# Where attention's results are read back to, and where one weight's low part comes from

## The chip, the cores and the metric

The kernel runs on one core of a Trainium2 chip. The metric is the device time of one execution in microseconds (us), less is better. TensorE is written PE (PEld is its weight load), VectorE DVE, ScalarE ACT, GpSimd POOL; SyncE, SP, issues the DMA transfers.

## The reference

One layer of a streaming encoder works on 1056 frames (1024 of a prompt and 32 of a sample) of 1024 features. Cut to what matters:

```
h  = rms_norm(x, g_mix);  z = h @ w_in            # q, k, v, ch, cb, cc, ga, gb
a  = window_attention(q, k, v) @ w_attn_out
bo = (cb * causal_conv3(cc * ch)) @ w_conv_out
x  = x + (sigmoid(ga) * a + sigmoid(gb) * bo) @ w_mix_out
x  = x + cross_attention(rms_norm(x, g_cross) @ w_cq, mem_k, mem_v) @ w_co
x  = x + square(relu(rms_norm(x, g_mlp) @ w_up)) @ w_down
```

A final norm follows. All inputs and results are float32.

## The kernel before, in words

Features lie on the 128 partitions, in eight groups (k on the input side of a product, f on the output side); frames run along a tile. The frames are cut into chunks c = 0, 1, 2 of 384, 384 and 288. To keep float32 accuracy on PE, every operand is held as a high part (its float32r rounding, by an ACT cast) and a low part (operand minus high part, a DVE subtract). A product of a 1024-feature input therefore takes 24 matmuls for one f and one chunk: for each k the weight's high part `wh` with the input's high part (L200), `wh` with the input's low part (L201) and the weight's low part `wl` with the input's high part (L202).

**Weights.** A list of steps is written out by hand, and each step names the weight it needs (`item`, `plan`, `worder`). `fetch_w` loads a 128 x 1024 weight (512 KB) into one of two raw tiles `wr` (L159); `issue_w` makes `wh` and `wl` from it (ACT L129, then DVE L130), up to three weights ahead. The weights of the output projections are used once for each chunk. For some of them, listed in the dictionary `kept`, the low part is written to HBM at the first use (`wl_d`, L179); at later uses only the cast is done (L173), and `wl` is read back from `wl_d` (L172). `w_conv_out` 1 is one of these.

**Stage 1, attention's output product.** Attention has stored its results in HBM (`ao_d`). `open_y` closes attention's memory pools and opens, in their memory, the gate pool `gb` (tags Gb0, Gb1 and Gb2 of five slots each) and the pools of the split operands `Y`. `load_attended(c, k)` reads group k of chunk c back and splits it: a DMA on SP (L788), a cast (L790), a subtract (L791). The read lands in a temporary tile `ct`, one of six (`NCT`) that the whole kernel shares. Chunk 0's eight reads come first; chunk 1's eight and the first four of chunk 2 are hung behind the three chunks of a gate product, and gates for chunk 2 follow (`gate_a2`, f = 2, 3, 4, with products in `pa` and results in Gb2). Then `do_attn_out(f)` takes f = 0 to 7; behind its first chunk at f = 0 hang the last four reads of chunk 2. Its product is scaled (L826) and stored (L827), or copied (L830). From f = 1 on, reads of the input use Gb0 and Gb1 (`gx_load`, L844); until then these two tags are empty, as the first gates live in another pool, `Ga`.

**Stage 2, the trunk.** Per chunk, `do_conv_out(c, f)` for eight f (DVE L1066 multiplies by the gate, POOL L1067 adds), then `do_mix(c, f)` for eight f (a read of x, L1077; L1081 adds it to the product; L279 and L280 scale and split, L276 sums squares on POOL), then cross attention. `do_conv_out(1, 0)` stands between chunk 0's conv products and its mix products; `do_conv_out(1, 1)`, the second use of `w_conv_out` 1, is the first step after chunk 0's last mix product. While the mix products run, reads and splits of cross attention's keys and values (L1092, L1105, L1097, L1109) are hung in between.

What is pinned keeps its written order; the rest is set by the language's scheduler, which decides on each engine's order from a model of time. Each engine, and SP's queue of DMA issues, works strictly in its order.

Of the kernel before, what the change touches and what calls it, by code (L numbers as in the profile page):

```python
# [10 lines left out]
F32 = mybir.dt.float32  # L11
# [11 lines left out]
CH = [(0, 384), (384, 384), (768, 288)]  # L23
# [17 lines left out]
def hybrid_step(ctx: ExitStack, tc: tile.TileContext, io):  # L41
# [5 lines left out]
    def nm(s):  # L47
        uid[0] += 1
        return f"{s}_{uid[0]}"
# [47 lines left out]
    def pin(ins):  # L97
        return tc.keep_in_program_order(ins)
# [6 lines left out]
    def tmp(n, dt=F32):  # L105
        return tp.tile([P, n], dt, tag="ct", bufs=NCT, name=nm("ct"))

    def slot(pool, tag, n, dt=F32R, bufs=None):
        return pool.tile([P, n], dt, tag=tag, bufs=bufs, name=nm(tag))
# [3 lines left out]

    plan, worder, kept = [], [], {}

    def item(fn, *keys):
        plan.append((fn, keys))
# [8 lines left out]
    def split(hi, lo, src):  # L128
        act.copy(hi, src)  # L129
        dve.tensor_sub(lo, src, hi.bitcast(F32))  # L130
# [16 lines left out]
    def fetch_w(raw=None):  # L147
        if raw is not None:
            pass
        elif third:  # L150
            third["n"] += 1
        if raw is not None:
            pass
        elif third and third["n"] % 3 == 0:
            raw = third["pool"].tile([P, 4, 256], F32, tag="ws", name=nm("wr3")).rearrange("p q c -> p (q c)")
        else:
            raw = wp.tile([P, 1024], F32, tag="wr", bufs=2, name=nm("wr"))
        src = weight(worder[wpos[0] + len(fetched)])
        load = sp.dma_start(raw.rearrange("p (i c) -> p i c", i=4) if len(src.shape) == 3 else raw, src)  # L159
        if third and third["n"] == 3 and third["pool"] is W["pool"]:  # L160
            pin(load)
        fetched.append(raw)

    def issue_w(pieces=(slice(0, 1024),)):
        if not fetched:
            fetch_w()
        raw = fetched.pop(0)
        key = worder[wpos[0]]
        hi = wp.tile([P, 1024], F32R, tag="wh", name=nm("wh"))
        lo = wp.tile([P, 1024], F32R, tag="wl", name=nm("wl"))  # L170
        if kept.get(key) is not None:
            sp.dma_start(lo.bitcast(F32), kept[key])  # L172
            act.copy(hi, raw)  # L173
        else:
            for at in pieces:
                split(hi[:, at], lo[:, at], raw[:, at])
            if key in kept:
                kept[key] = dram.tile([P, 1024], F32, name=nm("wl_d"))
                sp.dma_start(kept[key], lo.bitcast(F32))  # L179
        ready.append((worder[wpos[0]], (hi, lo)))  # L180
        wpos[0] += 1

    def next_w(key):
        while len(ready) <= LOOK and wpos[0] < len(worder) and worder[wpos[0]] is not STOP:
            issue_w()
        k, w = ready.pop(0)
        assert k == key, (k, key)
        return w
# [106 lines left out]
    def norm_x():  # L295
# [45 lines left out]
        with tc.manual_schedule(engines={mybir.EngineType.Activation, mybir.EngineType.DVE}):  # L341
            parts(0, range(1))
            issue_w((slice(0, 256), slice(256, 1024)))
            parts(0, range(1, NF))
            act.copy(ones_r, ones.to_broadcast([P, P]))
            issue_w()
            issue_w()
            squares(0)
# [115 lines left out]
    def do_K(pr, extras=()):  # L464
        def fn(w):
            kt = at_tile([P, NT], F32, "kt")
            ktt[pr] = kt
            for c, (o, n) in enumerate(CH):
                a = acc_tile([P, n])
                gemm(a, w, xg[c])  # L470
                dve.tensor_mul(kt[:, o : o + n], a, R[c])
                after(extras, c)
            sp.dma_start(io["o_k"][pr], kt[:, 896:])

        return fn
# [22 lines left out]
    def do_Q(kv, j, extras=()):  # L498
        def fn(w):
            for c, (o, n) in enumerate(CH):  # L500
                npr = min(n, NPR - o)
                if j == 0:
                    qs[kv, c] = at_tile([P, 4, npr], F32R, "QA" if c < 2 else "QB", 2 if c < 2 else 1)
                    if n > npr:
                        qs[kv, 3] = at_tile([P, 4, n - npr], F32R, "QC")
                a = acc_tile([P, n])
                gemm(a, w, xg[c])
                t = tmp(n)
                dve.scalar_tensor_tensor(t, a, 0.125, R[c], op0=ALU.mult, op1=ALU.mult)
                parts = [(qs[kv, c], slice(0, npr))]  # L510
                if n > npr:
                    parts.append((qs[kv, 3], slice(npr, n)))
                for q, s in parts:
                    for e in range(2):
                        own, other = slice(64 * e, 64 * e + 64), slice(64 - 64 * e, 128 - 64 * e)
                        h = 2 * j + e
                        act.copy(q[own, h], t[own, s])
                        dve.tensor_sub(q[other, h], t[own, s], q[own, h].bitcast(F32))
                after(extras, c)

        return fn
# [145 lines left out]
    G = {}  # L667
# [10 lines left out]
    def do_gate(to, extras=()):  # L678
        def fn(w):
            for c, (o, n) in enumerate(CH):  # L680
                a = acc_tile([P, n])
                gemm(a, w, xg[c])
                t = gate_slot(c, 0)
                dve.tensor_mul(t, a, R[c])
                act.activation(t, t, AF.Sigmoid)
                to(c, t)
                after(extras, c)

        return fn
# [61 lines left out]
    for i, h in enumerate(hosts):  # L751
# [16 lines left out]
        if h[0] == "Q":  # L768
            fn, key = do_Q(h[1], h[2], extras), qt(h[1], h[2])
        elif h[0] == "K":  # L770
            fn, key = do_K(h[1], extras), ("w_in", 8 + h[1])
        elif h[0] == "G":
            fn, key = do_gate(lambda c, t: sa.__setitem__((c, 0), t), extras), ("w_in", 34)
        else:
            fn, key = do_conv(*h, extras), conv_w(h[1], h[0])
# [7 lines left out]
    def yslot(c):  # L783
        return slot(Y[c if c < 2 else "top"], f"Y{c}", CH[c][1])

    def load_attended(c, k):
        t = tmp(CH[c][1])
        pin(sp.dma_start(t, ao_d[c][k // 2][:, k % 2]))  # L788
        hi, lo = aop[c][k] = (yslot(c), yslot(c))
        pin(act.copy(hi, t))  # L790
        pin(dve.tensor_sub(lo, t, hi.bitcast(F32)))  # L791
# [217 lines left out]
    item(open_y)  # L1009
    hold = lambda c, t: sg[c].__setitem__(0, t)  # L1010
    ao = lambda c, ks: [lambda k=k: load_attended(c, k) for k in ks]
    item(lambda: [e() for e in ao(0, range(NF))])
    b0 = [(0, e) for e in ao(1, range(4))] + [(1, e) for e in ao(1, range(4, NF))] + [(2, e) for e in ao(2, range(4))]
# [1007 lines left out]
```

## Time and profile before

| | |
|---|---|
| median of 3 runs | 1748.65 us (1747.12 to 1750.77) |
| profiled execution | 1748.9 us, its span 1746.4 us |
| granted TensorE clock | 0.998 |
| busy: PE, DVE, ACT, POOL | 99%, 68%, 49%, 34% |
| DMA | 346.60 MB, mean 198 GB/s |

Times of rows are in us from the start of the span. In a timeline row stand the start, the duration, engine, line, operation and output <- input; [idle before <- releaser] says how long the engine stood before it and what ended that, and xN joins N instructions in a row, whose first names the shape. A row of the waits names the waiting engine, its tile and line, what it waited for, and the total, the number and the longest. Stage 1 runs from about 540 to 650 us; the place in stage 2 is at 869.

### The profile page before, as it was taken

What the parts mean: (1) busy time and instruction counts of PE and PEld (TensorE: products, weight loads), DVE (VectorE), ACT (ScalarE), POOL (GpSimd) and SP (SyncE); (2) the same over time, 40 slices, a digit from 0 to 9 for tenths busy, and PEclk for the clock granted to TensorE, in tenths of its full rate; (3) what the DMA queues carried; (4) which work ended last, traced back from release to release, by engine and by line L of the source; (5) the groups of instructions that cost most, each with busy time, mean ns of one, the idle gap of its engine ahead of it and who ended that gap; (6) DMA issues with size and microseconds to landing.
All of it is one profiled execution on the core that took longest, in us unless ns stands there. A gap on an engine that the chain in (4) does not pass through costs nothing. (4 is left out here: it accounts for less than half of the span.)

```text
span 1746.4 us, 32603 instructions
## 1 busy us (share of the span) xinstructions
PE 1725.4 (99%) x12262; PEld 1708.0 (98%) x12262; DVE 1192.7 (68%) x2276; ACT 852.7 (49%) x1660; POOL 593.6 (34%) x667
## 2 busy tenths in 40 slices
PE   9999999999999999999999999999999999999998
PEld 8999999999999999999999999999999999999998
DVE  7776776867676656545677888787666686545675
ACT  8653533535335324434556666765444453333444
POOL 0026366453643444452225232005555410000121
PEclk9999999999999999999999999999999999999999
DMA  4333344333436888877766667775767695555555
GB/s 185 99 129 125 119 133 145 121 134 134 156 127 209 288 294 274 281 231 232 270 222 199 217 225 242 234 258 191 222 223 222 217 321 187 189 192 171 191 170 160
DMA packets 179854, 346.60 MB, mean 198 GB/s; under 512 B 18657, under 2 KB 101249, under 8 KB 179569
## 3 DMA queue, kind: packets, MB, share of 16 engines
q1 hardware_dynamic: 163504, 290.07, 50.5%
q0 software_dynamic: 15568, 53.68, 8.8%
q8 instruction: 96, 1.57, 0.4%
q10 hardware_dynamic: 624, 0.77, 0.1%
q14 instruction: 62, 0.50, 0.1%
HBM read 250.73 MB, written 93.14 MB: 197 GB/s over the span
## 5 line engine op out<-in xcount | busy, mean ns | idle before, releaser
L129 ACT CAST wh<-wr 128x1024 fp32r<-128x1024 f32 (+1 forms) x214 | 223.8, 1046 | 369.3 <-PE acc L1808 124.7
L130 DVE TENSOR_TENSOR wl<-wr,wh 128x1024 fp32r<-128x1024 f32 (+1 forms) x214 | 276.4, 1292 | 126.9 <-ACT wh L129 126.2
L200 PE MATMUL acc<-X,wh 128*128 128x384 f32 (+1 forms) x864 | 281.5, 326 | 0.0
L201 PE MATMUL acc<-X,wh 128*128 128x384 f32 (+1 forms) x864 | 278.6, 322 | 0.2 <-DVE X L280 0.2
L202 PE MATMUL acc<-X,wl 128*128 128x384 f32 (+1 forms) x864 | 277.8, 322 | 0.0
L276 POOL TENSOR_TENSOR xacc<-xacc,ct 128x384 f32<-128x384 f32 (+1 forms) x56 | 76.6, 1370 | 379.5 <-ACT ct L274 377.8
L201 PEld LDWEIGHTS acc<-X,wh 128*128 128x128 f32 x864 | 162.7, 188 | 1.5 <-DVE X L280 0.5
L200 PEld LDWEIGHTS acc<-X,wh 128*128 128x128 f32 x864 | 162.4, 188 | 0.9
L202 PEld LDWEIGHTS acc<-X,wl 128*128 128x128 f32 x864 | 162.4, 188 | 0.1
L200 PE MATMUL acc<-Y,wh 128*128 128x384 f32 (+1 forms) x432 | 139.4, 325 | 4.0 <-DVE ct L1066 2.9
L202 PE MATMUL acc<-Y,wl 128*128 128x384 f32 (+1 forms) x432 | 139.2, 323 | 1.8 <-DMA wl<-wl_d 1.8
L201 PE MATMUL acc<-Y,wh 128*128 128x384 f32 (+1 forms) x432 | 139.1, 323 | 0.0
L129 ACT CAST PTh<-pt 128x512 fp32r<-128x512 f32 (+3 forms) x94 | 45.8, 517 | 112.9 <-PE pt L598 111.6
L1807 PE MATMUL acc<-n,wh 128*128 128x264 f32 x352 | 100.2, 285 | 0.0
L1809 PE MATMUL acc<-n,wl 128*128 128x264 f32 x352 | 100.0, 285 | 0.2 <-DVE wl L130 0.2
L1808 PE MATMUL acc<-n,wh 128*128 128x264 f32 x352 | 100.1, 284 | 0.0
L735 POOL TENSOR_TENSOR ws<-ws 128x256 f32<-128x256 f32 x100 | 90.9, 909 | 5.6
L735 POOL TENSOR_TENSOR xacc<-xacc 128x256 f32<-128x256 f32 x100 | 88.9, 889 | 5.7 <-DMA xacc<-in_w_in 0.4
L200 PEld LDWEIGHTS acc<-Y,wh 128*128 128x128 f32 x432 | 80.8, 188 | 5.5 <-DVE ct L1066 3.8
L202 PEld LDWEIGHTS acc<-Y,wl 128*128 128x128 f32 x432 | 81.1, 188 | 2.2 <-DMA wl<-wl_d 2.2
L201 PEld LDWEIGHTS acc<-Y,wh 128*128 128x128 f32 x432 | 81.1, 188 | 0.1
L584 ACT ACTIVATE S<-S,nmx 128x257 f32<-128x257 f32 (+1 forms) x132 | 64.2, 488 | 18.9 <-DVE nmx L579 17.6
(432 smaller groups left out, 5553.7 us busy)
## 6 DMA issues: line engine op xcount, KB each, us to landing
wr<-in_w_up SPq DMA_DIRECT2D x53, 512.0 KB, 4.4
wr<-in_w_in SPq DMA_DIRECT2D x52, 512.0 KB, 3.6
wr<-wsum_d SPq DMA_DIRECT2D x40, 512.0 KB, 3.6
wr<-in_w_conv_out SPq DMA_DIRECT2D x24, 512.0 KB, 3.9
wr<-in_w_mix SPq DMA_DIRECT2D x24, 512.0 KB, 5.0
wr<-in_w_down SPq DMA_DIRECT2D x24, 512.0 KB, 4.1
n_d<-Z SPq DMA_DIRECT2D x32, 264.0 KB, 4.3
xacc<-in_w_down POOLq DMA_DIRECT2D x16, 512.0 KB, 4.6
```

What stands on the lines that cost most here:

```text
L129: act.copy(hi, src)
L130: dve.tensor_sub(lo, src, hi.bitcast(F32))
L200: pe.matmul(out, wh[:, a], hi, start=(k == 0), stop=False)
L201: pe.matmul(out, wh[:, a], lo, start=False, stop=False)
L202: pe.matmul(out, wl[:, a], hi, start=False, stop=(k == len(acts) - 1))
L276: pool_e.tensor_tensor(acc, acc, sq, op=ALU.add)
L584: act.activation(stl[:, h, : nk + 1], stl[:, h, : nk + 1], AF.Exp, scale=-1.0, bias=nmx[:, h : h + 1], accum_out=den[:, h : h + 1],)
L735: pin(pool_e.tensor_tensor(t[:, to], t[:, x], t[:, y], op=ALU.add))
L1807: pe.matmul(a, wh[:, s], hi, start=(t == 0 and k == 0), stop=False, skip_group_check=True)
L1808: pe.matmul(a, wh[:, s], lo, start=False, stop=False, skip_group_check=True)
L1809: pe.matmul(a, wl[:, s], hi, start=False, stop=(t == 1 and k == 7), skip_group_check=True)
```

## The change

In stage 1, reads of chunk 1 land in slots of Gb1 and those of chunk 2 in the first 288 columns of slots of Gb0, both idle then, instead of the six shared tiles. Chunk 0 stays with those. In the weights, a count of uses is kept; the second use of `w_conv_out` 1 forms its low part with the subtract L130, and only its third use reads it back.

```diff
-    plan, worder, kept = [], [], {}
+    plan, worder, kept, uses = [], [], {}, {}
...
-        if kept.get(key) is not None:
+        uses[key] = uses.get(key, 0) + 1
+        if kept.get(key) is not None and (key != ("w_conv_out", 1) or uses[key] == 3):
             sp.dma_start(lo.bitcast(F32), kept[key])
             act.copy(hi, raw)
         else:
             for at in pieces:
                 split(hi[:, at], lo[:, at], raw[:, at])
-            if key in kept:
+            if key in kept and uses[key] == 1:
                 kept[key] = dram.tile([P, 1024], F32, name=nm("wl_d"))
                 sp.dma_start(kept[key], lo.bitcast(F32))
...
     def load_attended(c, k):
-        t = tmp(CH[c][1])
+        t = slot(G["pool"], f"Gb{2 - c}", CH[2 - c][1], F32)[:, : CH[c][1]] if c else tmp(CH[c][1])
         pin(sp.dma_start(t, ao_d[c][k // 2][:, k % 2]))
```

Behind the added line all line numbers are one higher (L788 becomes L789). In the rows that follow, the number behind a name tells tiles apart.

SP in stage 1, from the seventh read of chunk 0 (`ao_d_3_80`) on; `ao_d_0_81` to `ao_d_3_84` are chunk 1, `ao_d_0_85` to `ao_d_3_88` chunk 2. Before:

```order
L788 DMA ct_6580<-ao_d_3_80 128x384
L788 DMA ct_6586<-ao_d_3_80 128x384
L788 DMA ct_6626<-ao_d_0_81 128x384
L788 DMA ct_6632<-ao_d_0_81 128x384
L159 DMA wr_6829<-in_w_attn_out 128x1024
L788 DMA ct_6638<-ao_d_1_82 128x384
```

and, after four more reads and a weight:

```order
L788 DMA ct_6696<-ao_d_3_84 128x384
L159 DMA wr_6998<-in_w_attn_out 128x1024
L788 DMA ct_6730<-ao_d_0_85 128x288
L788 DMA ct_6736<-ao_d_0_85 128x288
L788 DMA ct_6742<-ao_d_1_86 128x288
L788 DMA ct_6748<-ao_d_1_86 128x288
```

Now the same two places read:

```order
L789 DMA Gb_1104_6626<-ao_d_0_81 128x384
L789 DMA Gb_1107_6632<-ao_d_0_81 128x384
L789 DMA Gb_1110_6638<-ao_d_1_82 128x384
L789 DMA ct_6580<-ao_d_3_80 128x384
L789 DMA Gb_1113_6644<-ao_d_1_82 128x384
L789 DMA ct_6586<-ao_d_3_80 128x384
```

```order
L789 DMA Gb_1127_6696<-ao_d_3_84 128x384
L789 DMA Gb_1132_6730<-ao_d_0_85 128x288
L789 DMA Gb_1135_6736<-ao_d_0_85 128x288
L789 DMA Gb_1138_6742<-ao_d_1_86 128x288
L789 DMA Gb_1141_6748<-ao_d_1_86 128x288
L159 DMA wr_6998<-in_w_attn_out 128x1024
```

Three reads of chunk 1 have passed chunk 0's last two, and chunk 2's first four have passed a weight load. Its last four stand behind the first store of L827 (now L828) before and now.

PE at the first product of chunk 2 (`acc_6963`, f = 0) and of chunk 0 with the next weight (`acc_7004`, f = 1). Before (the second matmul of `acc_6963` stands right behind these rows):

```order
L202 MATMUL acc_6928<-Y_1128_6698,wl_6798 128x384
L200 MATMUL acc_6963<-Y_1133_6732,wh_6797 128x288
L200 MATMUL acc_7004<-Y_1076_6546,wh_6831 128x384
L201 MATMUL acc_7004<-Y_1077_6547,wh_6831 128x384
L202 MATMUL acc_7004<-Y_1076_6546,wl_6832 128x384
L200 MATMUL acc_7004<-Y_1079_6552,wh_6831 128x384
L201 MATMUL acc_7004<-Y_1080_6553,wh_6831 128x384
L202 MATMUL acc_7004<-Y_1079_6552,wl_6832 128x384
L200 MATMUL acc_7004<-Y_1082_6558,wh_6831 128x384
L201 MATMUL acc_7004<-Y_1083_6559,wh_6831 128x384
L202 MATMUL acc_7004<-Y_1082_6558,wl_6832 128x384
L200 MATMUL acc_7004<-Y_1085_6564,wh_6831 128x384
```

Now:

```order
L201 MATMUL acc_6963<-Y_1133_6732,wh_6797 128x288
L202 MATMUL acc_6928<-Y_1129_6699,wh_6797 128x384
L203 MATMUL acc_6928<-Y_1128_6698,wl_6798 128x384
L201 MATMUL acc_7004<-Y_1076_6546,wh_6831 128x384
L202 MATMUL acc_7004<-Y_1077_6547,wh_6831 128x384
L203 MATMUL acc_7004<-Y_1076_6546,wl_6832 128x384
L202 MATMUL acc_6963<-Y_1134_6733,wh_6797 128x288
L203 MATMUL acc_6963<-Y_1133_6732,wl_6798 128x288
L201 MATMUL acc_6963<-Y_1136_6738,wh_6797 128x288
L202 MATMUL acc_6963<-Y_1137_6739,wh_6797 128x288
L203 MATMUL acc_6963<-Y_1136_6738,wl_6798 128x288
L201 MATMUL acc_6963<-Y_1139_6744,wh_6797 128x288
```

The first matmul of `acc_6963` is two earlier, and three matmuls of `acc_7004`, not ten, stand before the other eleven that use the first four reads of chunk 2, which now follow without a break. Its last twelve come 26 matmuls after those, where before they were mixed with `acc_7004`'s. Ahead of all this, the first two matmuls of `acc_6869` and of `acc_6928` (f = 0, chunks 0 and 1) moved in front of the 24 of the gate product `pa_6835`.

DVE in stage 2, at `do_mix(0, f)` for f = 5 and 6, each of which has one L1081 (`mv` is a value of cross attention, `wl_10083` the low part of `w_conv_out` 1 in chunk 1). Before:

```order
L1109 TENSOR_TENSOR mv_10028<-mvr_10026,mv_10028 128x4x64
L1081 TENSOR_TENSOR Gb_1764_10066<-acc_10041,ct_10039 128x384
L280 SCALAR_TENSOR_TENSOR Y_1766_10069<-Gb_1764_10066,prm,Y_1765_10068 128x384
L1109 TENSOR_TENSOR mv_10077<-mvr_10075,mv_10077 128x4x64
L1081 TENSOR_TENSOR Gb_1775_10113<-acc_10088,ct_10086 128x384
```

Now:

```order
L1110 TENSOR_TENSOR mv_10028<-mvr_10026,mv_10028 128x4x64
L1082 TENSOR_TENSOR Gb_1764_10066<-acc_10041,ct_10039 128x384
L130 TENSOR_TENSOR wl_10083<-wr_1770_10080,wh_10082 128x1024
L281 SCALAR_TENSOR_TENSOR Y_1766_10069<-Gb_1764_10066,prm,Y_1765_10068 128x384
L1110 TENSOR_TENSOR mv_10077<-mvr_10075,mv_10077 128x4x64
L1082 TENSOR_TENSOR Gb_1775_10113<-acc_10088,ct_10086 128x384
```

One subtract came in. On SP, `L172 DMA wl_10083<-wl_d_9280 128x1024`, which stood ahead of the read into `ct_10086`, is gone.

## The prediction

> **What bounds the kernel now.** I read the page first, for the shares of the engines.
>
> ```profile
> span 1746.4 us, 32603 instructions
> PE 1725.4 (99%) x12262; PEld 1708.0 (98%) x12262; DVE 1192.7 (68%) x2276; ACT 852.7 (49%) x1660; POOL 593.6 (34%) x667
> ```
>
> TensorE (PE) is busy for 99% of the span. Work taken off another engine is therefore worth nothing in itself; time can go only where PE waits. The view of PE's waits comes next (total us, times, longest):
>
> ```profile
> PE acc L200 <- DVE ct L1066: 2.9, 3, 1.4
> PE acc L202 <- DMA wl<-wl_d: 1.8, 1, 1.8
> PE acc L200 <- ACT Y L790: 1.0, 2, 0.7
> ```
>
> The last two touch this change: a weight's low part read back from HBM, and, twice, the cast of an attention result that was read back. A pipelined engine also loses time as it restarts, so I size the three from the starts of the matmuls around them in PE's timeline (start, duration, idle before in brackets):
>
> ```profile
> 571.50 0.34 PE L202 MATMUL acc<-Y,wl 128*128 128x384 f32 x1
> 572.21 0.57 PE L200 MATMUL acc<-Y,wh 128*128 128x288 f32 x2 [0.38 <-ACT Y L790]
> 572.62 0.33 PE L201 MATMUL acc<-Y,wh 128*128 128x384 f32 x1
> ...
> 578.44 0.33 PE L202 MATMUL acc<-Y,wl 128*128 128x384 f32 x1
> 579.42 0.57 PE L200 MATMUL acc<-Y,wh 128*128 128x288 f32 x2 [0.65 <-ACT Y L790]
> 579.83 0.34 PE L201 MATMUL acc<-Y,wh 128*128 128x384 f32 x1
> ...
> 868.85 0.33 PE L200 MATMUL acc<-Y,wh 128*128 128x384 f32 x1
> 869.02 0.34 PE L201 MATMUL acc<-Y,wh 128*128 128x384 f32 x1
> 871.19 0.44 PE L202 MATMUL acc<-Y,wl 128*128 128x384 f32 x1 [1.84 <-DMA wl<-wl_d]
> 871.47 0.34 PE L200 MATMUL acc<-Y,wh 128*128 128x384 f32 x1
> ```
>
> Unhindered, 384-column matmuls start 0.17 us apart (868.85 to 869.02); for 288 columns I take 288/384 of that, 0.13. Each x2 row is one matmul of 288 columns and one of 384 (the order shows the second on another accumulator). So 0.47 should lie between the outer starts of the first two groups, where 1.12 and 1.39 do: 0.65 and 0.92 lost. The third takes 2.45 for two steps of 0.17: 2.11 lost. All three together are 3.68 us. A measurement of this kernel can tell about 0.2%, 3.5 us, from no change, so this is a change at the edge of what can be told.
>
> Why the reads of attention results are late is in SP's rows (its timeline, then its waits from 540 to 580 us) and in the windows (PE, PE load, DVE, ACT, POOL, clock, DMA share, GB/s):
>
> ```profile
> 543.26 12.78 SPq L788 DMA_DIRECT2D ct<-ao_d  x10
> 561.50 1.33 SPq L788 DMA_DIRECT2D ct<-ao_d  x2
> 566.11 2.27 SPq L788 DMA_DIRECT2D ct<-ao_d  x4
> 571.60 0.32 SPq L827 DMA_DIRECT2D m_d<-ct  x1
> 572.02 3.18 SPq L788 DMA_DIRECT2D ct<-ao_d  x4
> ...
> SPq L788 <- DVE Y L791: 11.1, 12, 5.5
> ...
> 550.00:556.00 6.00, 6.00 (x46) 6.00 (x45) 4.36 (x7) 4.37 (x9) 4.76 (x7) 1.00 0.49 144
> 556.00:578.00 22.00, 21.62 (x140) 21.20 (x139) 16.14 (x25) 10.32 (x21) 8.91 (x12) 1.00 0.99 343
> ```
>
> Six shared tiles take all 24 reads. SP stands up to 5.5 us until the subtract L791 frees one, while the DMA engines run at 0.49; afterwards they are full (0.99) and everything is late together.
>
> **The change, part by part.** First, the gate slots. Three reads of chunk 1 now stand ahead of the first read that waits for a shared tile. Each moves 128 x 384 x 4 bytes, 0.59 MB in all, 1.7 us at 343 GB/s; they move from the full stretch into the one with room. The four reads of chunk 2 that were issued from 566.11 need no shared tile and follow chunk 1's last reads (561.50 to 562.83) directly, so from 562.8 at the latest, and they pass the next weight load. Consumers and landings are these:
>
> ```profile
> 568.81 0.92 ACT L790 CAST Y<-ct 128x384 fp32r<-128x384 f32 x2
> 571.73 1.60 ACT L790 CAST Y<-ct 128x288 fp32r<-128x288 f32 x4 [1.99 <-DMA ct<-ao_d]
> 578.94 1.24 ACT L790 CAST Y<-ct 128x288 fp32r<-128x288 f32 x3 [5.61 <-DMA ct<-ao_d]
> 581.25 0.43 ACT L790 CAST Y<-ct 128x288 fp32r<-128x288 f32 x1 [1.07 <-DMA ct<-ao_d]
> 571.02 0.55 DVE L826 TENSOR_TENSOR ct<-acc,Ga 128x384 f32<-128x384 f32 x1
> 572.19 3.03 DVE L791 TENSOR_TENSOR Y<-ct,Y 128x288 fp32r<-128x288 f32 x4 [0.61 <-ACT Y L790]
> 579.40 1.26 DVE L791 TENSOR_TENSOR Y<-ct,Y 128x288 fp32r<-128x288 f32 x3 [3.52 <-ACT Y L790]
> DMA to landing us min/median/max: 1.9/5.2/7.3
> ```
>
> Issued 3.3 us earlier, the four land about 568 to 570 (562.8 to 564.1, four issues of 0.32, plus the median 5.2; 571.4 with the longest, 7.3). ACT is free at 569.7 and casts each in 0.4. DVE is free at 571.57, after L826, and needs 0.42 for a subtract (1.26 / 3), so the fourth low part is there at 573.3. That matters since the order now puts these four reads' matmuls in one block: PE reaches it at about 572.3 (571.50, two steps, three matmuls of the other accumulator) and wants the last low part at about 573.5. Before, ten other matmuls lay between the first and the second of them; that cover is gone, and 0.2 us is left. Were the subtracts as slow as the 0.76 of 572.19 (3.03 / 4), the fourth would come at 574.6 and PE lose 1.1. With before's times (575.22) it would lose 1.7. I take 0.1, nearest to the 0.42 row.
>
> The last four reads still stand behind the store L827, but their slots do not wait for the same subtracts: the first fills an idle fifth slot, the others follow the first block's subtracts, about 572 to 573.3 in place of 572.02 to 575.20. With 1.7 us less ahead in the DMA engines the first lands at 577.2 instead of 578.94, is cast at 577.6, and PE wants it at about 578.2 (578.61, two matmuls later in the order, less the 0.65 gained). The last, 581.25 less 1.9, is there by 579.4 at the latest and wanted at about 579.5, cast included: between nothing and 0.5 lost, for me 0.1. Four matmuls of this stage also move ahead of a gate's 24; their data, chunk 1's first read, is one of the three early ones, cost nil. ACT and DVE do the same casts and subtracts as before. Stage 1 gives 0.65 + 0.92 - 0.2 = 1.37.
>
> Second, the low part formed afresh. The read (512 KB, SP) goes, one DVE subtract comes, ACT's cast stays. Its place:
>
> ```profile
> 864.74 0.85 SPq L172 DMA_DIRECT2D wl<-wl_d  x1
> 866.59 1.05 ACT L173 CAST wh<-wr 128x1024 fp32r<-128x1024 f32 x1 [3.75 <-DMA wr<-in_w_conv_out]
> 861.39 1.22 DVE L130 TENSOR_TENSOR wl<-wr,wh 128x1024 fp32r<-128x1024 f32 x1
> 867.06 0.56 DVE L1081 TENSOR_TENSOR Gb<-acc,ct 128x384 f32<-128x384 f32 x1 [2.77 <-DMA ct<-in_x]
> 871.72 0.56 DVE L1081 TENSOR_TENSOR Gb<-acc,ct 128x384 f32<-128x384 f32 x1 [1.61 <-DMA ct<-in_x]
> 868.83 1.01 POOL L276 TENSOR_TENSOR xacc<-xacc,ct 128x384 f32<-128x384 f32 x1 [4.82 <-ACT ct L274]
> 961.12 1.97 DVE L130 TENSOR_TENSOR wl<-wr,wh 128x1024 fp32r<-128x1024 f32 x1 [0.55 <-ACT wh L129]
> ```
>
> The cast ends at 867.64, L1081 ahead of it on DVE at 867.62. The subtract then takes 1.22, to 868.86; PE wants the low part at 869.19 (869.02 + 0.17). The wait of 2.11 goes, with 0.3 to spare. The subtract pushes the rest of DVE's row back by 1.2; DVE idles 1.61 before 871.72, and the read of x that ends this wait has 512 KB less ahead of it (1.5 us at 343 GB/s), so that covers it. The raw tile is held 1.2 us longer, to the subtract's end, and with it the next weight load on SP. I put 0.1 on what this leaves. Without the cover each would show up to 1.2.
>
> An L130 took 1.97 at 961.12, not 1.22. The Trainium skill, "SBUF — State Buffer", section "Who interferes with whom", says that a DVE operation with two SBUF inputs and a GpSimd operation that reads SBUF hold one port pair by turns, the other blocked; that speaks against adding an L130, and the two durations are in line with it. By the rows themselves, POOL starts only at 868.83 here, so I take 1.22; at 1.97 the low part would be there at 869.61 and 0.42 of the wait would stay.
>
> Sum: 3.68 - 0.2 - 0.1 = 3.4 us. The profiled execution took 1748.9 in all (span 1746.4 and 2.5 around it), so 1745.5; against the median of the runs, 1748.65, it is 1745.2.
>
> **The rivals.** A, only part goes: the last chunk-2 reads stay behind the store L827 and PE still waits near 578, or DVE, which ends waits of 2.9 us later (L1066), gives the time back there. For: 572.02 follows 571.60 directly. Against: PE starts the stretches in which DVE leads. Without the 0.92 or with as much lost: 1746.2; with only the second stage, 1746.6; with only the first, 1747.3.
>
> B, slower: the block of twelve matmuls. SP issues in order, and the new reads wait for memory that the closed attention pools held, on PE, ACT, POOL, where the shared tiles waited on DVE alone. If one stands there d longer, all reads and weight loads behind it are late by d, and PE, which has nothing between the block's matmuls, loses d - 0.2. The gain of 3.4 is eaten at d = 3.6; slower by over 0.2% from d = 7.1, near 1752.2 or more. For: SP's waits of 5.5 show that it does stand so long, and the new waits have no row before. Against: d must exceed 5.5, the longest wait seen.
>
> C, more: the waits on L1066 shrink as PE comes earlier against DVE and POOL. If one of the longest, 1.4, went too, 1743.8. For: their phase can move either way; against: nothing in the change aims there.
>
> That the fresh part brings nothing is A's 1747.3: if the raw weight landed 2 us later than before (for it, the wait of ACT for it, 3.75; against it, SP issues it no later).
>
> **How the numbers follow.** Main case 0.50, at 1745.2, its own range 1744.2 to 1746.2, half of it beyond 1745.15 (0.2% faster): 0.25 faster, 0.25 same. C 0.20, faster. A 0.13, same. B 0.17, slower, more than its rows say because the new waits are unseen. Faster 0.45, same 0.38, slower 0.17. The range leaves B out and little of C: 1743.0 (C with 0.8 more of those waits) to 1749.5 (A with nothing gained and a subtract's 0.8 lost).
>
> **What would show it.** Right: no PE wait on L791's cast near 572 and 578, none on wl at 869, three reads into gate slots before 550, chunk 2's first four reads issued by 564, the new subtract near 868 in 1.2 us, later waits as before. Wrong: a PE wait inside the block near 573 (B), a read into a gate slot that holds SP past 553 (B), a wait at 578 still (A), a subtract of 2 us (leftover 0.4), waits on L1066 of another size (A or C).

## The result, and the profile after

Over 22 runs each, the median is 1747.78 us against 1750.68 before; the ratio of the two is 0.9985, 95% interval 0.9979 to 0.9992. That is 0.15%, 2.6 us less (1.4 to 3.7). The forecast was 3.4 us less; its sign and its range hold, its terms don't all.

The page of the changed kernel (span, then busy time):

```profile
span 1744.4 us, 32597 instructions
PE 1727.6 (99%) x12262; PEld 1711.1 (98%) x12262; DVE 1192.0 (68%) x2277; ACT 852.8 (49%) x1660; POOL 593.2 (34%) x667
```

The span is 2.0 us shorter and PE is busy 2.2 us longer: PE waits less but some of its work runs slower (at a lower clock, as shown below). The view of PE's waits no longer has the two rows that the forecast was about. Its largest row is the old one, one line lower:

```profile
PE acc L201 <- DVE ct L1067: 3.1, 3, 1.5
```

Stage 1, SP's timeline (start of the issue, duration, tile), the windows (the column before the last is the DMA share), and PE's timeline at the last four reads of chunk 2:

```profile
545.88 2.74 SPq L789 DMA_DIRECT2D Gb<-ao_d  x3
560.88 3.55 SPq L789 DMA_DIRECT2D Gb<-ao_d  x5
570.61 0.33 SPq L828 DMA_DIRECT2D m_d<-ct  x1
570.99 2.02 SPq L789 DMA_DIRECT2D Gb<-ao_d  x4
...
556.00:578.00 22.00, 22.00 (x144) 22.00 (x143) 15.89 (x27) 10.46 (x23) 10.02 (x12) 1.00 0.91 302
...
579.31 0.29 PE L203 MATMUL acc<-Y,wl 128*128 128x288 f32 x1
579.50 0.40 PE L201 MATMUL acc<-Y,wh 128*128 128x288 f32 x1
580.00 0.41 PE L202 MATMUL acc<-Y,wh 128*128 128x288 f32 x1
```

Three reads of chunk 1 are issued from 545.88 to 548.62. Chunk 1's last and chunk 2's first four go out from 560.88 in one row, where the four alone began at 566.11 before. The full stretch is no longer full (0.91, was 0.99). PE is busy through all of it; the time still lost is behind it, at the last read's two operands: from 579.31 to 580.00, two steps of 0.13 took 0.69.

Stage 2, DVE and PE:

```profile
863.84 1.23 DVE L130 TENSOR_TENSOR wl<-wr,wh 128x1024 fp32r<-128x1024 f32 x1
...
866.86 0.34 PE L202 MATMUL acc<-Y,wh 128*128 128x384 f32 x1
867.04 0.34 PE L203 MATMUL acc<-Y,wl 128*128 128x384 f32 x1
```

The fresh low part is there at 865.07 and PE takes it at 867.04 without a pause. (In the second trace of this kernel, shown below, it does not.) The price shows 20 us later, on ACT, DVE and PE, where R's row for cross attention is made:

```profile
878.07 0.41 ACT L129 CAST mkh<-mkr 128x256 fp32r<-128x256 f32 x1 [2.81 <-DMA mkr<-in_cmem_k]
878.51 0.43 DVE L130 TENSOR_TENSOR mkl<-mkr,mkh 128x256 fp32r<-128x256 f32 x1 [1.99 <-ACT mkh L129]
...
886.35 0.33 PE L201 MATMUL acc<-Y,wh 128*128 128x384 f32 x1
886.83 0.44 PE L250 MATMUL pr<-ct,ones_r 128*128 128x384 f32 x1
```

A step of 0.48 instead of 0.17 stands there; before, PE found the operand ready, and ACT had waited less for the same key:

```profile
881.25 0.41 ACT L129 CAST mkh<-mkr 128x256 fp32r<-128x256 f32 x1 [1.88 <-DMA mkr<-in_cmem_k]
```

### The profile page after: what moved, and what is told of

It is laid out like the page before. It is cut to its first block, busy times and chain, and to the rows that moved or that the text cites. A ratio compares the mean times of both kernels' runs of the same rounds, so it can differ in the third digit from the quotient of the medians.

```text
span 1744.4 us, 32597 instructions
## 1 busy us (share of the span) xinstructions
PE 1727.6 (99%) x12262; PEld 1711.1 (98%) x12262; DVE 1192.0 (68%) x2277; ACT 852.8 (49%) x1660; POOL 593.2 (34%) x667
## 5 line engine op out<-in xcount | busy, mean ns | idle before, releaser
L130 DVE TENSOR_TENSOR wl<-wr,wh 128x1024 fp32r<-128x1024 f32 (+1 forms) x215 | 277.6, 1291 | 117.7 <-ACT wh L129 116.8
```

## The experiments

**Each edit alone.** The first kernel has only the new slots (`t = slot(...)` in `load_attended`), the second only the fresh low part (`uses`).

> Only the reads of chunks 1 and 2 go to gate slots; the low part is read back as before. Theory: the two edits act in separate places. The two waits on the cast near 571 and 578 go, up to 0.3 us left at the fourth late read, about 1.2 us in all; the waits near 676 to 685 shrink by 0.66 as in the full change if stage 1 alone causes that; the wait of 2.1 at 869 stays. PE is 1.9 us ahead of the kernel before at 860, and the time is 1.9 us (0.1%) less. Rival: the 0.66 near 680 is chance of one execution, then PE is 1.2 ahead there.

> Only the fresh low part; all reads go through the six shared tiles. Theory: the waits near 571 and 578 stay at 0.65 and 0.92, the wait at 869 goes whole (2.1 us), and 0.5 us comes back near 890 where R's row is made, so PE is 1.6 us ahead at 910 and the time 1.6 us (0.09%) less. Rival: the 0.5 near 890 is there only because stage 1 already put PE ahead of the loads of the memory keys; then it is nearer to nothing here and the gain 2.1.

Measured, 12 runs each: slots alone 0.9996 (0.9984 to 1.0007), fresh part alone 0.9995 (0.9986 to 1.0004). Neither is told from no change, so these times cannot divide the gain; traces must. They brought a surprise. Up to 864 us the second kernel has the matmuls and the DMA issues of the kernel before, in the same order, yet the wait at 579 is not there; and in the first, where the low part is still read back, the wait for it is 0.23 us, not 1.84:

```profile
866.82 0.44 PE L202 MATMUL acc<-Y,wl 128*128 128x384 f32 x1 [0.23 <-DMA wl<-wl_d]
```

**So: is the first trace typical?** The kernel before and the changed one were each run twice more, unchanged.

> The kernel before once more, for a second trace. Theory (the waits on reads of attention results differ from one execution to the next, as the run with the fresh low part alone, the same instructions up to 864 us, had no wait at 578): the waits near 571 and 578 add up to anything from 0.4 to 1.6 us, the wait at 869 is 1.5 to 2.5 each time, and stretches of lower granted clock after 990 us cost 0 to 5 us. Rival (the first trace is typical): 0.65, 0.92 and 2.1 again, no stretch of lower clock.

> The kernel before a third time. Theory and rival as for the second: waits near 571 and 578 of 0.4 to 1.6 us in all, 1.5 to 2.5 at 869, lower clock costing 0 to 5 us after 990; the rival expects the first trace's numbers again.

> The changed kernel once more, for a second trace. Theory: none or up to 0.4 us of wait near 579 as in the first, none at 869, 0.3 to 1.1 us given back near 887; stretches of lower clock after 990 us cost 0 to 5 us as in the kernel before. Rival (fuller PE brings the clock down): more of them than in the kernel before, in every execution.

> The changed kernel a third time; theory and rival as for its second trace: at most 0.4 us near 579, none at 869, 0.3 to 1.1 us near 887; lower clock costing 0 to 5 us by theory, always more than in the kernel before by the rival.

It is not. PE's timeline in the second trace of the kernel before, in its third, then in the second trace of the changed kernel:

```profile
572.52 0.58 PE L200 MATMUL acc<-Y,wh 128*128 128x288 f32 x2 [0.27 <-ACT Y L790]
579.35 0.58 PE L200 MATMUL acc<-Y,wh 128*128 128x288 f32 x2 [0.25 <-ACT Y L790]
871.47 0.44 PE L202 MATMUL acc<-Y,wl 128*128 128x384 f32 x1 [2.94 <-DMA wl<-wl_d]
```

```profile
579.17 0.57 PE L200 MATMUL acc<-Y,wh 128*128 128x288 f32 x2 [1.01 <-ACT Y L790]
869.87 0.44 PE L202 MATMUL acc<-Y,wl 128*128 128x384 f32 x1 [1.34 <-DMA wl<-wl_d]
```

```profile
866.71 0.44 PE L203 MATMUL acc<-Y,wl 128*128 128x384 f32 x1 [0.45 <-DVE wl L130]
```

The read-back's wait is 0.23, 1.34, 1.84 and 2.94 in four traces, a wider spread than the 1.5 to 2.5 expected. The changed kernel missed its bounds too: in the second trace the low part came from a subtract that started only at 865.43, and PE waited 0.45 for it where none was expected. PE always has the same matmuls in the same stretch, so the time between the starts of the same two of them, taken from each trace, says what a stretch cost, waits and clock together:

| stretch (times of the first trace) | shared tiles or read-back | the change, or its part for this stretch |
|---|---|---|
| 567.8 to 590.1, 130 matmuls (stage 1) | 22.32, 21.77, 22.05, 21.39 | 21.17, 21.15, 20.65, 21.36 |
| 865.4 to 879.5, 70 matmuls (low part) | 14.09, 16.69, 13.53, 12.48 | 12.85, 11.92, 13.48, 12.05 |
| 879.5 to 903.5, 140 matmuls (R's row) | 23.98, 23.98, 23.98, 23.89 | 25.04, 24.50, 24.59, 25.36 |

(On the left the kernel before three times and, as fourth, the one with the other edit alone; on the right, in the first row, slots alone and the changed kernel three times, in the others fresh part alone and the changed kernel three times.) The slots give 0.80 on the mean. Two kernels further below, with the keys pinned and with every low part fresh, issue the same matmuls and DMAs as the changed kernel throughout stage 1; they took 22.19 and 20.65, which makes it 0.69 and lets the two sides overlap. PE's timeline in the first of them has the wait that the forecast said would go:

```profile
578.63 0.41 PE L201 MATMUL acc<-Y,wh 128*128 128x288 f32 x1 [0.34 <-ACT Y L791]
```

So a gain of the slots is likely, but it is not clear of the scatter. The fresh part gives 1.62 at its place (0.8 without the 16.69, in which the clock sank; 1.2 with the clock's 1.6 taken out of it, below) and loses 0.91 at R's row, more than nothing in each of these traces but unevenly: 0.5 to 1.4, and 0.2 to 1.1 in the four later kernels that have the fresh part and keep the split of the key there. Net, by these means, it is worth 0.7 at most and perhaps nothing. Other places vary as much without any part in the change: 400 matmuls from 650 to 717 us took 67.55, 66.52 and 67.00 in the kernel before and 66.88, 66.66 and 66.45 in the changed one, so the 0.66 near 680 that the first expectation asks about is chance, as its rival had it.

**The clock.** Until PE's last matmul, the first trace of the kernel before had no stretch of lower granted clock; every other trace had some, mostly at the same places between 990 and 1150. The windows of the third trace of the kernel before, of its second, then of the changed kernel's first (clock third from the end):

```profile
1130.00:1140.00 10.00, 10.00 (x74) 10.00 (x73) 6.78 (x19) 5.48 (x15) 1.12 (x2) 0.83 1.03 389
```

```profile
870.00:880.00 10.00, 8.53 (x40) 8.53 (x41) 7.85 (x11) 4.97 (x9) 2.93 (x3) 0.83 0.57 202
```

```profile
1070.00:1080.00 10.00, 9.10 (x53) 8.08 (x52) 7.11 (x18) 6.15 (x15) 0.00 (x0) 0.83 0.57 210
1130.00:1140.00 10.00, 10.00 (x74) 10.00 (x73) 6.54 (x20) 6.00 (x14) 0.00 (x0) 0.83 0.96 378
```

The 0.83 is the mean of a window of 10 us. Narrower windows of the second of these traces show what it is made of:

```profile
872.00:873.00 1.00, 1.00 (x7) 1.00 (x6) 0.91 (x2) 0.31 (x1) 0.00 (x0) 0.80 0.16 62
873.00:874.00 1.00, 1.00 (x5) 1.00 (x4) 1.00 (x2) 1.00 (x4) 0.14 (x1) 0.50 0.08 30
874.00:875.00 1.00, 1.00 (x5) 1.00 (x4) 1.00 (x2) 0.97 (x2) 1.00 (x1) 0.50 0.29 53
875.00:876.00 1.00, 1.00 (x5) 1.00 (x4) 1.00 (x3) 0.03 (x1) 0.18 (x1) 0.50 0.85 332
876.00:877.00 1.00, 1.00 (x8) 1.00 (x7) 1.00 (x2) 1.00 (x3) 0.00 (x0) 1.00 0.54 188
```

The clock stood at 0.50 for 3.4 us, from 872.6 to 876.0, and matmuls of 384 columns there start 0.32 us apart instead of 0.17. Such a drop costs about 1.6 us: ten steps are 0.15 longer here, and 0.5 x 3.4 = 1.7 would be its full share. The changed kernel's first trace has two, some 3.2 us, and the kernel before had none in the trace it is compared with, so that is where its span lost what its waits had gained. The rival of these four runs, that a fuller PE brings the clock down, does not hold for this change: in one batch of runs the mean clock was 0.9956 before (23 runs), 0.9958 with slots alone and 0.9962 with the fresh part alone; in another 0.9958 before (25 runs) and 0.9957 with the change and earlier reads. (The last two kernels below, from that batch, had 0.9953 and 0.9950; why is open.) At one clock, 0.996, the means were 1749.24 before (5 runs), 1747.64 with the slots (7) and 1749.97 with the fresh part (6) in the first batch, 1749.32 before (16) and 1747.56 with the change and earlier reads (6) in the second. That puts the gain with the slots, about 1.7 us; with a scatter of 1 to 1.7 us between runs of one clock it is an indication and no proof. It is more than the 0.7 to 0.8 that stage 1 shows, and what makes up the rest of the 2.6, whose interval begins at 1.4, is open.

**Which reads carry stage 1?** Chunk 1's alone into gate slots (`if c == 1 else tmp(...)`), and chunk 2's alone (`if c == 2`).

> The full change, but chunk 2's reads go through the shared tiles; only chunk 1's go to gate slots. Theory (the early reads of chunk 1 relieve the shared tiles and the full stretch of the DMA engines): chunk 2's first four are still read by 565 and both waits go, PE within 0.3 us of the full change at 600. Rival (chunk 2's own slots do it): its reads wait for shared tiles, the first wait stays or grows to some 1.7 us, since the block of twelve matmuls without cover stands in this order too.

> The full change, but chunk 1's reads go through the shared tiles; only chunk 2's go to gate slots. Theory (chunk 1's early reads take 1.7 us out of the full stretch): chunk 2's first four come earlier than before as they need no shared tile, so the first wait (0.65) goes, but the late four land later than in the full change and the second wait stays, 0.5 to 0.9. Rival (chunk 2's slots alone do it): both waits go, PE within 0.3 us of the full change at 600.

Windows of the kernel before, then of the first, then of the second, with DVE's, POOL's and PE's timeline of the second:

```profile
546.00:556.00 10.00, 10.00 (x70) 10.00 (x70) 5.35 (x10) 5.16 (x11) 5.19 (x7) 1.00 0.65 208
```

```profile
546.00:556.00 10.00, 10.00 (x70) 10.00 (x69) 4.91 (x9) 4.69 (x10) 5.20 (x7) 1.00 0.85 288
556.00:578.00 22.00, 22.00 (x145) 22.00 (x145) 16.84 (x28) 10.99 (x24) 10.76 (x12) 1.00 0.95 315
```

```profile
546.00:556.00 10.00, 10.00 (x72) 10.00 (x71) 5.39 (x10) 5.47 (x12) 5.19 (x7) 1.00 0.67 208
556.00:578.00 22.00, 21.77 (x141) 21.53 (x140) 17.46 (x27) 10.90 (x24) 9.71 (x12) 1.00 0.98 344
571.54 2.99 DVE L792 TENSOR_TENSOR Y<-Gb,Y 128x288 fp32r<-128x288 f32 x3
571.64 3.49 POOL L736 TENSOR_TENSOR xacc<-xacc 128x256 f32<-128x256 f32 x4
574.59 0.40 PE L202 MATMUL acc<-Y,wh 128*128 128x288 f32 x1 [0.23 <-DVE Y L792]
```

With chunk 1's reads early, the DMA engines are at 0.85 where SP stood waiting before and they ran at 0.65, and stage 1 takes 20.65, as little as in any trace, though chunk 2 still goes through the shared tiles. With chunk 2's slots alone it takes 21.21 and PE waits inside the block, not at 579 as the theory had it. This points to chunk 1's slots, but it is one trace each, and both times lie within what the changed kernel itself took. The second kernel also shows the forecast's slow subtract, 1.0 us each at 571.54 instead of 0.42, while POOL works.

**The last four reads ahead of the store.**

```diff
+        g = (2 - c) if c == 1 or k < 4 else 1
+        t = slot(G["pool"], f"Gb{g}", 384, F32)[:, : CH[c][1]] if c else tmp(CH[c][1])
...
-    ... + [(2, e) for e in ao(2, range(4))]
+    ... + [(2, e) for e in ao(2, range(NF))]
```

> The full change, and chunk 2's last four reads too are hung on the gate product, into Gb1 slots, so that they are issued ahead of the first store instead of behind it. Theory: PE's last lost time of stage 1 (0 to 0.7 us near 579 in the traces of the changed kernel) comes from these four landing late; it goes, stage 1 takes 35.1 us for the matmuls from 568 to 581 at most 0.1 more than the least seen, and the time is 0.4 us less than the changed kernel's. Rival: the earlier reads push back the next weight load or the first four, and a wait of 0.5 us or more appears near 572 or on a weight after 581.

Its stage 1 takes 20.67 and has no wait. That fits these reads, behind the store L828, being what the changed kernel sometimes loses at 579; but the changed kernel got 20.65 without this edit in one of its traces, so one trace does not show it. In time, 0.9996 of before (0.9985 to 1.0007, 10 runs), the 0.4 us can't be seen. This kernel holds the whole change, and its ratio alone is not told from no change either.

**What holds R's row.** In `mem_key`, casts and subtracts of the sample's keys keep their written order too (`if bufs == 4:` becomes `if True:`); the scheduler had pulled them forward from the last chunk's cross attention.

> The full change, and the splits of the sample's memory keys keep their written order, so that they leave the stretch from 870 to 890 where the scheduler had put them. Theory: the low part formed afresh lets PE catch up with the chain that makes R's row, and this chain stands on such a split (waiting for the read of a key) on DVE; with it gone the matmuls from 879 to 903 take 24.0 us as in the kernel before, not 24.5 to 25.4, and PE is 0.5 to 1.4 us further ahead at 903. Rival: the chain is held by POOL's sums or by DVE's other work, and 24.5 or more stays. Later, near 1030 to 1050, the splits may cost something in their new place.

The fresh part's stretch takes 11.92, as little as in any trace, and R's row 23.98, as in the kernel before. PE's timeline:

```profile
886.61 0.34 PE L250 MATMUL pr<-ct,ones_r 128*128 128x384 f32 x1
```

So the loss at R's row goes with DVE standing at the split of a key whose read is not yet there: with the split gone from that place, so is the loss, in this one trace. The other traces fit. Where the low part is read back, DVE stood 0.7 to 1.1 us before the second of these splits and nothing was lost; with the fresh part and the split there it stood 1.1 to 2.1 us and 0.2 to 1.4 was lost, though the two do not go in step. The kernel as a whole took 1.0005 of before (0.9995 to 1.0014): the scheduler moved much of the later cross attention with it. A better kernel is not shown.

**More of the same.** Every kept weight formed afresh in the second chunk (`uses[key] == 3` as the whole condition), seven subtracts more and seven reads fewer.

> The full change, but the low part is formed afresh in the second chunk for every kept weight that is still read back there, seven subtracts more. Theory: only w_conv_out 1 had a wait on its read, so nothing is gained; where DVE leads (near 890 and from 950 to 1000) each subtract of 1.2 us shows in part, and PE loses 1 to 4 us from 879 to 992 against the changed kernel. Rival (reads of low parts load the DMA engines, so fewer are better): PE gains 0.5 us or more there.

It is slower, 1.0019 of before (1.0010 to 1.0029). From 879 to 992 it takes 113.71 (25.07 + 88.64) against 112.87, 112.79 and 113.61 in the changed kernel's three traces, so it loses 0.1 to 0.9, less than expected; the larger part, 3.5 to 4 us up to 1055 without the clock's share, is behind it, in PE's waits from 985 to 1060:

```profile
PE o L1198 <- ACT PTh L129: 1.8, 1, 1.8
PE acc L201 <- DVE ct L1067: 0.9, 2, 0.7
PE o L1198 <- DVE PTl L130: 0.7, 1, 0.7
PE acc L1225 <- DVE Ga L1229: 0.6, 1, 0.6
```

The first, third and fourth are not in the changed kernel's stretch. Fewer bytes did not pay for the DVE time. Part of the 0.0019, some 1.2 us of 3.3, goes with the lower mean clock of its runs, 0.9950 against 0.9958 before.

## Why the prediction was right, and where not

- Direction and range were right, and in stage 1 the mechanism: three reads by 549, the first four of chunk 2 by about 564 (in a row from 560.88 to 564.43), no wait near 572 in any of the three traces, cover of the block sufficient. Its size was not: 1.37 was forecast, 0.7 to 0.8 came. The step that failed is the first one, "0.65 and 0.92 lost": these were one execution's, and against the least time of the stretch, 20.65, the four traces of these instructions lost 0.74 to 1.67. The changed kernel's instructions lost 0 to 0.7, and 1.5 in one trace.
- The leftover at the last read was inside its bounds ("between nothing and 0.5") in the first trace, 0.4, and outside them in the third, 0.7. A's place, behind the store, was right.
- Stage 2: the subtract took 1.23 and the wait of 2.11 went, as worked out, though a wait of 0.45 for the subtract stood in the second trace. "I put 0.1 on what this leaves" is the step that was mis-sized: 0.9 came back at R's row. It named the right causes, DVE's row and the loads on SP, but took their idle time near 871 as cover, and did not follow them to the next place where PE needs DVE. PE, 2 us earlier, arrives before the key's read. DVE giving the time back is what rival A said, but at R's row and not at L1066: the outcome is nearer to A with only the first stage than to the main case.
- C's gain at L1067 did not come (3.1, 3.1 and 3.0 in the changed kernel's traces, 2.9, 3.2 and 3.4 before). B's waiting SP came only in small: three issues of 0.33 took 2.74 at the first gate slots, 1.8 us of standing, far below B's 5.5, and the reads behind still went out in time.
- That the total came near the forecast is partly luck. The two places add up to 1.5 us at most by their traces, not 3.4, and the 2.6 holds more than they explain. The median, 1747.78, lies above the main case's own range of 1744.2 to 1746.2, as the kernel before came out at 1750.68 and not at the 1748.65 of three runs. Faster by over 0.2% was its likeliest outcome, at 0.45; 0.15% is less than that.
- The Trainium skill's rule on the shared port ("SBUF — State Buffer", "Who interferes with whom") did not decide here: POOL began at 865.03, when the new subtract was near its end. In the kernel with chunk 2's slots alone the subtracts of 1.0 us beside POOL agree with it.

## What to carry to other kernels

A wait of 1 to 2 us on a transfer is one draw: before it goes into a sum, take it from several executions, and compare the time between the same two instructions in each. A wait removed on the busiest engine moves that engine earlier against all the others; the gain counts only once the next place where they meet is passed. Starting reads while the transfer engines have room seemed worth more here than giving the late reads their own space, by one trace each. And a share read over a window is a mean: narrow the window before calling it a state.

## What the runs showed of the hardware

The granted clock falls to 0.50 for 3.4 us at a time (twice for 6.8 us), none to four times in a trace before PE's last matmul, often at the same places of the program, with and without the change. A drop of 3.4 us costs about 1.6 us, which fits the 1.5 us of time that go with 0.001 of a run's mean clock (51 runs of the kernel before, fitted). Of the 27 drops in the 13 traces, 15 began within 8 us behind a PE wait of 0.4 us or more, as the one at 872.6 behind the wait of 2.94 that ended at 871.47; the other 12 stand between 1132 and 1142 without one. But most such waits have no drop behind them: the one near 1040 is in all 13 traces, and a drop follows it in 6. What sets a drop off is not shown. At this size of change the mean clock belongs beside every time.
